# A hybrid decoder trunk: the attention's branch product two query/key stages later, gate weights one stage earlier, embedding transposes later

## The chip, the core and the metric

The kernel runs on one core of a Trainium2 chip. The metric is the device time of one execution in microseconds (us). TensorE (PE; its weight loads PEld) multiplies, ScalarE (ACT) and VectorE (DVE) work element by element, GpSimd (POOL) does a few small steps, and SyncE (SP) issues the transfers from memory.

## The reference

Two layers over 256 tokens of width 1024; all inputs are float32. Cut to what matters here:

```python
h = h + 0.5 * swiglu(rmsnorm(h, ffn1_norm), ...)
u = rmsnorm(h, mix_norm);  z = u @ w_in     # split: m_qk, m_v, m_o, m_i, m_f, a_q, a_k, a_v, g_m, g_a
m_qk = silu(causal_dwconv(m_qk))            # 4 taps
hm = sigmoid(m_o) * headnorm(mlstm(m_q, m_k, m_v, m_i, logsigmoid(m_f)))    # 4 heads of 256
ha = sliding-window attention with sinks(norm(a_q), norm(a_k), a_v)         # 16 heads of 64, window 128
h = h + (sigmoid(g_m) * (hm @ w_branch_m) + sigmoid(g_a) * (ha @ w_branch_a)) @ w_out
h = h + 0.5 * swiglu(rmsnorm(h, ffn2_norm), ...)
h = h + sigmoid(rmsnorm(h, ple_norm) @ ple_gate_w) * (p_i @ ple_proj_w)
```

## The kernel before

Every float32 operand of a large product is split in two: a high part (a cast on ScalarE, `wh` for weights) and a low part (a subtraction on VectorE, `wl`). A product is then three matmuls per tile: high by high, high by low, low by high. Weights come in megabytes: SP loads one into one of two `raw` buffers, and ScalarE and VectorE split each half of it into one of eight ring slots of `wh` and `wl`. A raw buffer is loaded again when its second half is split.

The order of the instructions on TensorE, ScalarE, VectorE and SP is written by the program while it is built. `self.jobs` holds the stages in turn: each is a function that issues one stage's matmuls. Side work runs in chains (generators), of which one step is issued between matmuls when `Clock`, the planner's own estimate of every engine's time, says that its input is ready; `tick` looks for such steps. Weight splits are issued in the same way (`feed`). So a stage that is moved in `jobs` also moves the loads of its weights on SP, their splits, and the places of the chains around it. A wait in the chip comes where the planner's clock was too early.

In the mixer (`mix`) the stages of one layer are, with the tile names of the profile: `kvq` (attention keys, values and queries), `v` (the recurrence's values), `gt` (merge gate A), `if` (input and forget gates, `log_gates`), `ya` (the attention's branch product), `z` twice (the recurrence's queries and keys of heads 0 and 1, each followed by the chain `conv`), `og` (output gate), `z` twice (heads 2 and 3), `gt` (merge gate M), `ym`, `yo`.

Chains that run beside them: the attention groups (`sc` scores, `pr` probabilities, `tp` their transposes, `ptd` the split transposes, `ha` the outputs, which are split into the tiles `qT`, the operand of `ya`); `scans`, from the `if` product through Exp and Ln and VectorE's scans to `gcols` and `rows`; `decays` (`wt`, then Exp into `w`); `conv` (`cv` taps, `cy` the Silu, `qk` its split); and one `head` per head (`st`, `num`, `og`, `tp`, `hmT`). The matmuls of `if` take a 128x1024 tile `wif`, which `gate_weights` (line 905) clears on POOL and fills with two casts and two subtractions.

In the last block of a layer (`ple`) the embedding `p` is loaded by a prelude that the down product before it calls when it begins. `later_T` schedules p's transposes; its last argument is the earliest time by the planner's clock.

## Time and profile before

| | us |
|---|---|
| median of 3 runs (1392.11 to 1394.45) | 1393.32 |
| profiled execution | 1395.02 |
| its span, first to last instruction | 1393.2 |
| TensorE busy | 1371.4 |
| ScalarE busy | 726.7 |
| VectorE busy | 862.3 |

The mean granted TensorE clock is 0.997. In the rows that follow, a line of a timeline is start, duration, engine, what is written from what, the form, the count, and in brackets the idle time just before and what ended it. A row of stretches has the width, then the busy time of TensorE, its weight loads, VectorE, ScalarE and GpSimd with the instructions in brackets, then the granted clock, the share of the transfer engines, and GB/s. All instructions that the planner records have line 130.

### The profile page before, as it was taken

How to read it: one execution, taken by the hardware profiler on the slowest of the kernel's cores; microseconds unless marked ns; L12 is line 12 of the kernel's file. 1: busy time of each engine (PE TensorE's matmuls, PEld its weight loads, DVE VectorE, ACT ScalarE, POOL GpSimd, SP SyncE). 2: the span in 40 equal slices, each digit the busy share in tenths (PEclk: the TensorE clock that was granted, in tenths of full speed). 3: DMA queues.
4: the chain of work that ended last, by engine and by line, in shares of the span. 5: the costliest groups of instructions: out<-in, count | busy, mean ns of one | idle time of the engine just before them, and what ended most of it. 6: DMA issues, size and time to landing. Idle time of an engine off the chain costs nothing.

```text
span 1393.2 us, 21942 instructions
## 1 busy us (share of the span) xinstructions
PE 1371.4 (98%) x9056; PEld 1236.9 (89%) x9056; DVE 862.3 (62%) x1213; ACT 726.7 (52%) x1138; POOL 55.0 (4%) x84
## 2 busy tenths in 40 slices
PE   8999999999999999999999999999999999999998
PEld 5999887899899889988779998878998998999886
DVE  5655457765886665554575554586658876555544
ACT  5555346874665454443554443477756554544433
POOL 0000012000000000000000000120000000000000
PEclk9999999999999999999999999999999999999999
DMA  6665645464545565565456566455445554655551
GB/s 209 218 210 167 228 136 196 124 149 151 168 152 182 166 212 186 169 229 182 165 164 210 172 207 208 143 164 145 135 134 192 173 160 161 227 191 170 205 181 61
DMA packets 125830, 243.81 MB, mean 175 GB/s; under 512 B 14977, under 2 KB 23841, under 8 KB 125730
## 3 DMA queue, kind: packets, MB, share of 16 engines
q1 hardware_dynamic: 125730, 242.41, 54.6%
q8 instruction: 71, 1.16, 0.4%
q14 instruction: 29, 0.24, 0.0%
HBM read 241.34 MB, written 1.05 MB: 174 GB/s over the span
## 4 chain that ended last, share of the span: by engine, by line
PE 90%; DMA 3%; DVE 3%; ACT 2%; issue 1%; POOL 0%; SPq 0%; ACTq 0%; POOLq 0%
PE dn L130 16%; PE pg L130 15%; PE pu L130 14%; PE gu L130 7%; PE z L130 7%; PE gt L130 6%; PE ya L130 4%; PE ym L130 3%; PE v L130 3%; PE og L130 3%; PE yo L130 3%; PE kvq L130 3%; PE tp L130 2%; PE sc L130 1%; DVE wl L130 1%; PE ha L130 1%
## 5 line engine op out<-in xcount | busy, mean ns | idle before, releaser
L130 DVE TENSOR_TENSOR wl<-raw,wh 128x1024 fp32r<-128x1024 f32 (+1 forms) x448 | 540.8, 1222 | 365.8 <-ACT wh L130 364.7
L130 ACT CAST wh<-raw 128x1024 fp32r<-128x1024 f32 x448 | 461.5, 1050 | 439.8 <-PE dn L130 86.9
L130 PE MATMUL dn<-wh,hid 128*128 128x512 f32 x688 | 218.4, 395 | 0.0
L130 PE MATMUL pg<-uT,wh 128*128 128x256 f32 x1088 | 194.6, 281 | 0.0
L130 PE MATMUL pu<-uT,wh 128*128 128x256 f32 x1088 | 193.6, 281 | 0.0
L130 PEld LDWEIGHTS pg<-uT,wh 128*128 128x128 f32 x1088 | 167.1, 189 | 0.2
L130 PEld LDWEIGHTS pu<-uT,wh 128*128 128x128 f32 x1088 | 166.9, 188 | 0.0
L130 PEld LDWEIGHTS dn<-wh,hid 128*128 128x128 f32 x688 | 129.3, 188 | 29.9
L130 PE MATMUL pg<-uT,wl 128*128 128x256 f32 x544 | 152.9, 281 | 0.0
L130 PE MATMUL pu<-uT,wl 128*128 128x256 f32 x544 | 152.9, 281 | 0.0
L130 PE MATMUL dn<-wl,hid 128*128 128x512 f32 x352 | 138.7, 394 | 0.0
L130 PEld LDWEIGHTS pu<-uT,wl 128*128 128x128 f32 x544 | 102.5, 188 | 0.0
L130 PEld LDWEIGHTS pg<-uT,wl 128*128 128x128 f32 x544 | 102.4, 188 | 0.0
L130 PE MATMUL gt<-uT,wh 128*128 128x256 f32 x512 | 93.2, 283 | 0.0
L130 PE MATMUL z<-uT,wh 128*128 128x256 f32 x512 | 92.1, 282 | 0.0
L130 PE MATMUL gu<-wh,uT 128*128 128x512 f32 x256 | 83.5, 402 | 1.9 <-ACT uT L130 1.9
L130 PEld LDWEIGHTS gt<-uT,wh 128*128 128x128 f32 x512 | 79.0, 188 | 1.2
L130 PEld LDWEIGHTS dn<-wl,hid 128*128 128x128 f32 x352 | 66.2, 188 | 15.3
L130 PEld LDWEIGHTS z<-uT,wh 128*128 128x128 f32 x512 | 78.7, 188 | 0.2
L130 PE MATMUL z<-uT,wl 128*128 128x256 f32 x256 | 72.0, 281 | 0.0
L130 PE MATMUL gt<-uT,wl 128*128 128x256 f32 x256 | 71.9, 281 | 0.0
L130 PE MATMUL kvq<-wh,uT 128*128 128x512 f32 x192 | 63.7, 401 | 0.0
(194 smaller groups left out, 2034.2 us busy)
## 6 DMA issues: line engine op xcount, KB each, us to landing
raw<-in_w_in_dram SPq DMA_DIRECT2D x60, 1024.0 KB, 5.1
raw<-in_ffn_w_up_dram SPq DMA_DIRECT2D x40, 1024.0 KB, 5.2
raw<-in_ffn_w_down_dram SPq DMA_DIRECT2D x40, 1024.0 KB, 5.5
raw<-in_ffn_w_gate_dram SPq DMA_DIRECT2D x39, 1024.0 KB, 5.7
raw<-in_w_branch_a_dram SPq DMA_DIRECT2D x16, 512.0 KB, 5.9
raw<-in_w_branch_m_dram SPq DMA_DIRECT2D x8, 1024.0 KB, 5.1
raw<-in_w_out_dram SPq DMA_DIRECT2D x8, 1024.0 KB, 5.1
raw<-in_ple_gate_w_dram SPq DMA_DIRECT2D x8, 1024.0 KB, 7.3
```

Of the source, the lines that this page charges most:

```text
L130: return issue(*args, **kw)
```

## The change

Three edits. The two query/key jobs of heads 0 and 1 are put ahead of the attention's branch product instead of behind it, so that `ya` stands two `z` stages farther back. `gate_weights` becomes a job of its own ahead of the gate stage, and keeps its tile in `w_if`, where `log_gates` takes it. And p's transposes may start 15 us after their issue by the planner's clock, not 5.

```diff
-                self.later_T(p[:, t, :], pT, 0, t, 2, self.clock.now + 5.0)
+                self.later_T(p[:, t, :], pT, 0, t, 2, self.clock.now + 15.0)
...
+        self.jobs.append(rec.gate_weights)
         ga = gate(C_GA)
 
         self.jobs.append(rec.log_gates)
+        for part in range(2):
+            rec.qk_job(w_in, part, 0)
...
         job_T(units_a, att.haT, "ya", use_a, lambda: self.finish(groups[0]))
 
-        for part in range(2):
-            rec.qk_job(w_in, part, 0)
         units_o = self.pair(w_in, C_O)
...
-        return w
+        self.w_if = w
 
     def log_gates(self):
         tr, nc = self.tr, self.nc
-        w = self.gate_weights()
-        ps = tr.bank("if")[:, :T]
+        w, ps = self.w_if, tr.bank("if")[:, :T]
```

On TensorE in layer 0, around the last attention outputs (`ha`) before the change; `qT26` and `qT28` are the high and the low part of the second half of their split result, `qT25` and `qT27` of the first half.

```order
L130 MATMUL ya578_3165<-qT25_136,wl553_2990 128x256
L130 MATMUL ha585_3229<-ptd588_3253,vpad368_1994 128x512 x3
L130 MATMUL ha585_3229<-ptd589_3255,vpad368_1994 128x512 x3
L130 MATMUL tp597_3340<-ident_79,gates572_3159 128x4
...
L130 MATMUL ya575_3162<-qT26_137,wh555_3013 128x256
L130 MATMUL ya575_3162<-qT28_139,wh555_3013 128x256
L130 MATMUL ya575_3162<-qT26_137,wl556_3014 128x256
```

And after it; the rows left out are the rest of the second `z` job with the gates' transposes and three of the `wt`, and then the first half of `ya` with the fourth.

```order
L130 MATMUL z578_3163<-uT6_117,wl554_2993 128x256
L130 MATMUL ha580_3185<-ptd587_3271,vpad368_1994 128x512 x3
L130 MATMUL z595_3335<-uT5_116,wh556_3015 128x256
...
L130 MATMUL ya614_3503<-qT25_136,wh584_3228 128x256
L130 MATMUL ya614_3503<-qT27_138,wh584_3228 128x256
...
L130 MATMUL ya614_3503<-qT26_137,wh605_3422 128x256
L130 MATMUL ya614_3503<-qT28_139,wh605_3422 128x256
```

The last `ha` moved from five small transposes ahead of the first reader of `qT26` to a whole `z` job and half of `ya` ahead of it.

On ScalarE at the same place before the change, from the split of that `ha` result through the decays (`em` and `w` are Exp).

```order
L130 CAST qT26_137<-ha585_3229 128x4x128
L130 ACT_TABLE_LOAD
L130 ACTIVATE em600_3358<-gcols598_3346 128x8
L130 ACTIVATE w602_3370<-wt601_3360,gcols598_3346 128x128 x3
L130 CAST wh604_3390<-raw594_3320 128x1024
L130 ACTIVATE w602_3370<-wt603_3386,gcols598_3346 128x128 x3
```

And after it, with the Silus of the convolutions (`cy`) of the moved jobs.

```order
L130 CAST qT26_137<-ha580_3185 128x4x128
L130 ACT_TABLE_LOAD
L130 ACTIVATE em602_3394<-gcols600_3366 128x8
L130 ACTIVATE w604_3412<-wt603_3396,gcols600_3366 128x128 x3
L130 CAST wh605_3422<-raw592_3313 128x1024
L130 ACT_TABLE_LOAD
L130 ACTIVATE cy608_3435<-cv593_3329 128x512
L130 ACT_TABLE_LOAD
L130 ACTIVATE w604_3412<-wt607_3431,gcols600_3366 128x128 x3
L130 ACT_TABLE_LOAD
L130 ACTIVATE cy609_3453<-cv594_3332 128x512
L130 CAST qk610_3467<-cy608_3435 128x512
```

The Exp of the decays and the Silu of the convolutions now alternate, with a table load at each turn; in all there are 18 table loads in the program where 10 were.

On TensorE in the down product before `ple` in layer 0 before the change, the transposes of `p`:

```order
L130 MATMUL dn1021_6444<-wh996_6264,hid41_152 128x512
L130 MATMUL dn1021_6444<-wl997_6265,hid41_152 128x512
L130 MATMUL dn1021_6444<-wh996_6264,hid47_158 128x512
L130 MATMUL tp1027_6482<-ident_79,p1017_6439 128x128 x2
L130 MATMUL tp1028_6485<-ident_79,p1017_6439 128x128 x2
```

and after it:

```order
L130 MATMUL dn1021_6444<-wh1009_6369,hid42_153 128x512
L130 MATMUL dn1021_6444<-wl1010_6370,hid42_153 128x512
L130 MATMUL dn1021_6444<-wh1009_6369,hid48_159 128x512
L130 MATMUL tp1037_6550<-ident_79,p1017_6439 128x128 x2
L130 MATMUL tp1038_6553<-ident_79,p1017_6439 128x128 x2
```

They stand 48 matmuls of the down product farther back. On SP the load of `p` stays where it was; in the mixer the four megabytes for the two moved `z` jobs are now loaded ahead of the four for `ya`.

## The prediction

> **What bounds the kernel now.** First the page: the span, the engines and the chain that ended last.

> ```profile
> span 1393.2 us, 21942 instructions
> PE 1371.4 (98%) x9056; PEld 1236.9 (89%) x9056; DVE 862.3 (62%) x1213; ACT 726.7 (52%) x1138; POOL 55.0 (4%) x84
> PE 90%; DMA 3%; DVE 3%; ACT 2%; issue 1%; POOL 0%; SPq 0%; ACTq 0%; POOLq 0%
> ```

> TensorE works 98% of the span and carries 90% of the chain, so a change in order that adds and removes no matmul can win only what TensorE loses: its idle 21.8 us (1393.2 less 1371.4), and time at a reduced clock, which hides inside "busy". Next the list of TensorE's waits (us in total, times, longest) for the waits that the change touches.

> ```profile
> PE ya L130 <- DVE qT L130: 2.7, 2, 1.3
> PE tp L130 <- DMA p<-in_p_dram: 2.1, 2, 1.7
> PE sc L130 <- DVE ptd L130: 0.9, 2, 0.5
> PE ya L130 <- ACT qT L130: 0.6, 2, 0.3
> PE if L130 <- DVE wif L130: 0.4, 2, 0.2
> ```

> All come in pairs, one per layer. Four of the five belong to the three edits: `ya` (the branch product), `if` (the gate weights' product), `tp` from `p` (the embedding transposes). These lists count idle time from the modelled end of a matmul; what a stall costs must be taken from start to start, and its stage looked at for the clock.

> **The branch product.** Timeline of TensorE in layer 0 (start, duration), then stretches (width, busy per engine, granted clock), then both for layer 1.

> ```profile
> 319.52 0.38 PE L130 MATMUL ya<-qT,wh 128*128 128x256 f32 x1 [0.28 <-ACT qT L130]
> 321.25 0.39 PE L130 MATMUL ya<-qT,wh 128*128 128x256 f32 x1 [1.34 <-DVE qT L130]
> ...
> 321.30:322.50 1.20, 1.20 (x9) 1.10 (x10) 0.00 (x0) 0.05 (x1) 0.00 (x0) 0.91 0.57 97
> 322.50:324.00 1.50, 1.50 (x8) 1.50 (x8) 0.00 (x0) 0.83 (x3) 0.00 (x0) 0.50 1.00 380
> 324.00:326.00 2.00, 2.00 (x13) 2.00 (x11) 0.00 (x0) 0.00 (x0) 0.00 (x0) 0.57 0.48 185
> 335.70:358.40 22.70, 22.70 (x193) 22.70 (x193) 15.19 (x21) 12.47 (x17) 0.00 (x0) 1.00 0.48 154
> ...
> 1008.61 0.39 PE L130 MATMUL ya<-qT,wh 128*128 128x256 f32 x1 [0.28 <-ACT qT L130]
> 1010.34 0.39 PE L130 MATMUL ya<-qT,wh 128*128 128x256 f32 x1 [1.34 <-DVE qT L130]
> 1011.50:1013.00 1.50, 1.50 (x11) 1.50 (x10) 0.00 (x0) 0.88 (x3) 0.00 (x0) 0.59 0.95 348
> 1013.00:1015.00 2.00, 2.00 (x11) 2.00 (x10) 0.00 (x0) 0.06 (x1) 0.00 (x0) 0.50 0.57 222
> 1015.00:1020.00 5.00, 5.00 (x43) 4.71 (x43) 2.73 (x4) 3.59 (x8) 0.00 (x0) 0.98 0.01 3
> ```

> A 256-column matmul takes its turn every 0.118 us (22.70 for 193, in the stage after). In layer 0 the second half of `ya` waits 0.28 for the high part of qT, and from 319.52 to 321.25 for the low part: 1.73 less 0.118 is 1.61. Right behind it the clock falls: 1.20 x 0.09 + 1.50 x 0.50 + 2.00 x 0.43 = 1.72 lost. Layer 1: 0.28, 1.73 less 0.118 = 1.61, and 1.50 x 0.41 + 2.00 x 0.50 + 5.00 x 0.02 = 1.72. Together 3.61 a layer, 7.2 us, twice what the list of waits shows.

> After the change two query/key jobs (384 matmuls, 45 us) stand between the gate product and `ya`. The last `ha`, which makes qT's second half, is issued in the middle of them, and `ya` first reads that half 23 us later. So this stall goes, and I count all of its 7.2.

> [...]

> **The gate weights.** Two casts (ScalarE) and two subtractions (VectorE) on 128x32 move from just ahead of the `if` product to the start of the gate stage, with POOL's 128x1024 memset.

> ```profile
> 300.81 0.28 PE L130 MATMUL gt<-uT,wl 128*128 128x256 f32 x1
> 301.31 1.19 PE L130 MATMUL if<-uT,wif 128*128 128x256 f32 x8 [0.21 <-DVE wif L130]
> 989.87 0.28 PE L130 MATMUL gt<-uT,wl 128*128 128x256 f32 x1
> 990.38 1.19 PE L130 MATMUL if<-uT,wif 128*128 128x256 f32 x8 [0.23 <-DVE wif L130]
> ```

> Start to start 0.50 and 0.51, less 0.118: 0.38 and 0.39, 0.8 us together. In their new place they stand ahead of ScalarE's exponentials of scores. They are 0.34 us of work there, and ScalarE idles 0.58 before its next cast of a transposed tile, as the two rows of ScalarE's timeline say (the first in its old place):

> ```profile
> 300.59 0.34 ACT L130 CAST wif<-wif 128x32 fp32r<-128x32 f32 x2
> 272.34 0.59 ACT L130 CAST ptd<-tp 128x512 fp32r<-128x512 f32 x1 [0.58 <-PE tp L130]
> ```

> so the push ends there, and I cost it at nothing; without that cover it would come back as at most 0.34 a layer. POOL's memset takes another buffer of the pool, which the order shows free since a transpose in the value stage, ahead of the whole gate stage; on POOL's queue nothing stands behind it until the heads' powers in the output-gate stage.

> **The embedding transposes.** They go back from 5 to 15 us behind p's load by the planner's clock; in the order that is 48 matmuls of 512 columns.

> ```profile
> 611.95 0.40 PE L130 MATMUL dn<-wh,hid 128*128 128x512 f32 x1
> 612.75 0.63 PE L130 MATMUL tp<-ident,p 128*128 128x128 f32 x4 [0.40 <-DMA p<-in_p_dram]
> 1300.96 0.40 PE L130 MATMUL dn<-wh,hid 128*128 128x512 f32 x1
> 1303.03 0.63 PE L130 MATMUL tp<-ident,p 128*128 128x128 f32 x4 [1.68 <-DMA p<-in_p_dram]
> ...
> 1303.73 0.39 PE L130 MATMUL dn<-wl,hid 128*128 128x512 f32 x1
> 1303.96 0.63 PE L130 MATMUL dn<-wh,hid 128*128 128x512 f32 x2
> ```

> A 512-column matmul turns in 0.235 (1303.73 to 1303.96 and its like), so the losses are 0.80 less 0.235 = 0.57, and 2.07 less 0.235 = 1.84: 2.4 us. 48 of them are 11.3 us of new cover against 1.84: the wait goes. p's load itself keeps its place on SP's queue; pT is first read by the next block, behind the whole down product, so its cast and subtraction have room.

> **What it adds.** The matmuls are the same. ScalarE now meets the Exp of the decays between the Silus of the convolutions: the order has 7 table loads in each mixer stage where 3 were, 18 against 10 in all.

> ```profile
> L130 ACT ACT_TABLE_LOAD x10 | 12.8, 1283 | 10.0 <-DVE cv L130 5.3 <-PE gu L130 3.9 <-PEq L1271 0.7
> 319.49 1.28 ACT L130 ACT_TABLE_LOAD   x1
> 320.78 0.21 ACT L130 ACTIVATE em<-gcols 128x8 f32<-128x8 f32 x1
> L130 ACT CAST wh<-raw 128x1024 fp32r<-128x1024 f32 x448 | 461.5, 1050 | 439.8 <-PE dn L130 86.9
> L130 DVE TENSOR_TENSOR wl<-raw,wh 128x1024 fp32r<-128x1024 f32 (+1 forms) x448 | 540.8, 1222 | 365.8 <-ACT wh L130 364.7
> L130 DVE SCALAR_TENSOR_TENSOR cv<-z,feat,cv 128x255 f32<-128x255 f32 (+2 forms) x96 | 44.9, 480 | 8.1 <-ACT cv L130 5.8
> raw<-in_w_in_dram SPq DMA_DIRECT2D x60, 1024.0 KB, 5.1
> 372.59 2.00 ACT L130 CAST wh<-raw 128x1024 fp32r<-128x1024 f32 x2 [2.46 <-DMA raw<-in_w_in_dram]
> ```

> Four more are 5.1 us of ScalarE a layer, and some loads hold the queue until VectorE has done its taps (0.48 each). What is late next? I walked the new order of layer 0 with these durations. `if` now starts at 300.93 and ends at 303.3. The query job takes 22.7 for its products and 3 for the `ha` and `tp` between; the last `ha` stands at 317.5 and its operand is subtracted at 314.3 (VectorE does the gate scans until 312.5, then one wl and the subtraction): 3.2 to spare. The `ya` job starts at 331.0 and reads qT's second half from 342.7; that is written at 322.9. ScalarE's stretch with the loads begins at 320.4: load and `em` 321.8, first decays (their `wt` ends at 322.5) and a wh 324.4, load and Silu 326.2, load and decays 328.3, load, Silu and a cast 330.7, four `cv` 332.6, load and decays 334.6, a cast and wh of `ya`'s sixth part 336.2. VectorE, held by twelve taps until 337.5 and one subtraction, has its wl at 339.3, wanted at 345.5: 6.2 to spare. The low part of the first keys (343.0) is wanted by `st` at 348.4: 5.4. The first output-gate weights are split at 347.6, wanted at 356.7. So the loads cost nothing on TensorE. Their cover is these 5.4 us, about one layer's extra loads again.

> The SP queue now loads four megabytes of query/key weights ahead of the four branch weights. With two raw buffers and 5.1 us a landing the branch weights arrive 10 us or more before `ya`.

> Behind that the heads of the recurrence stand closer to their inputs, and the walk finds little room: 1.5 us at the first head's transpose in the output-gate stage and at the third head's `st`, 1.2 at its `num`, about 0 at the second head's transpose (388.1 against 388.05). A landing that is 2.46 late, as the last row shows ScalarE waiting, would turn one of these into a wait. Bounds: nothing; or a wait like `ya`'s, 3.6 a layer. Since most margins are over 1 us I take 0.5 a layer, near the small `sc` wait (0.9 for two).

> **Sum** against the profiled execution (1395.02, of which the span is 1393.2): -7.2 - 0.8 - 2.4 + 1.0 = -9.4, so 1385.6. The median of the runs shown, 1393.32, is 1.7 below that execution; by the same step it becomes 1383.9, and I say 1384.0.

> **Rivals.**

> First, the slow clock does not belong to the wait of `ya`, and strikes elsewhere. For it: in layer 1 TensorE lost 1.84 at p's transposes, as much as at `ya`, and the clock stayed. [...] Against: both layers show it 0.9 to 1.2 us behind `ya`'s wait, nowhere else in a busy stretch. Then 3.4 of the gain stays out: 1387.3.

> Second, one of the heads' thin margins becomes a wait of 1.6 us and drags the clock down again, in each layer: 7.2 back in place of my 1.0, so 1390.1. For it: the margins of 0 to 1.5; against: the same chains stand in the order of before, and the list of waits has none of their tiles.

> Third, the change doesn't do what it says: `ya` waits for something new, such as its own later weights, 5 us a layer. 1393.3 less 10.4 plus 10 is 1393, no difference.

> Fourth, slower: ScalarE's added table loads. If the queue runs later than the 6.2 and 5.4 of cover, `ya` and `st` wait for it, us for us, with 1.7 of slow clock. To lose 3 us in all it must eat 10.4 + 3, 6.7 a layer, hence run some 10 us later than walked, twice the 5.1 that the loads take. Time 1396 to 1398. [...]

> **Chances.** The forecast as it stands 0.66, the clock rival 0.09, the heads' waits 0.12, no effect 0.07, slower 0.06. The measurement of this kernel can tell about 0.2% (2.8 us). The heads' case lies at 3.2 and is split, 0.10 faster and 0.02 same: faster 0.85, same 0.09, slower 0.06. Range: the top takes in the heads' case, 1390.2; the bottom has no new wait (1.0), the two `sc` waits gone by shift (0.9), and 1 of the runs' spread (1392.11 to 1394.45): 1381.0.

> **What would show it.** Right: no wait of `ya` for qT, clock 1.00 through both `ya` stages, `if` 0.118 behind the last `gt`, no wait for p; 18 table loads; spans shorter by 3 to 4 a layer in the mixer. Wrong: a new TensorE wait of over 1 us on `hmT`, `og`, `num`, `st` or `wl` in the mixer, or a clock under 0.9 there.

## The result, and the profile after

The changed kernel takes 1381.52 us (median of 5 runs, 1379.98 to 1383.27) against 1392.52 for the kernel before (5 runs, 1391.37 to 1394.45): a ratio of 0.992, 95% interval 0.9907 to 0.9934. That is 11.0 us less, where 9.4 were forecast (1384.0, range 1381.0 to 1390.2). It is faster, and a little more than said. The times of the kernel before that follow leave out one run of the first set, which took 2248.49 us at a granted clock of 0.558.

The page of the changed kernel, its first lines and the shares of the chain that ended last:

```profile
span 1381.5 us, 21941 instructions
PE 1366.2 (99%) x9056; PEld 1233.3 (89%) x9056; DVE 860.7 (62%) x1213; ACT 734.8 (53%) x1146; POOL 55.4 (4%) x84
PE 96%; DMA 1%; DVE 1%; ACT 1%; issue 0%; POOL 0%; SPq 0%; ACTq 0%; POOLq 0%
```

The matmuls are as many as before. TensorE's idle time went from 21.8 to 15.3 us (1381.5 less 1366.2), and its busy time fell by 5.2, though no matmul was removed. That part is pace (how closely the matmuls follow each other), the clock (0.997 granted before, 0.998 after) and short gaps that count as busy. Next its waits, the whole list (us in total, times, longest):

```profile
PE tp L130 <- DVE xn L130: 3.9, 2, 3.0
PE g L130 <- DVE pick L265: 2.4, 1, 2.4
PE gu L130 <- ACT uT L130: 2.2, 1, 2.2
PE sc L130 <- DVE ptd L130: 0.9, 2, 0.5
PE gu L130 <- DVE wl L130: 0.8, 1, 0.8
```

The waits of `ya` for qT, of `if` for wif and of `tp` for p are gone, all three, and no wait of the heads (`hmT`, `og`, `num`, `st`) came. At the places themselves, from TensorE's timeline and, for `ya`, the stretches from its start to the output gate in both layers:

```profile
300.92 0.28 PE L130 MATMUL gt<-uT,wl 128*128 128x256 f32 x1
301.04 0.40 PE L130 MATMUL if<-uT,wif 128*128 128x256 f32 x2
...
331.53 0.40 PE L130 MATMUL ya<-qT,wh 128*128 128x256 f32 x2
331.77 0.28 PE L130 MATMUL ya<-qT,wl 128*128 128x256 f32 x1
331.50:357.40 25.90, 25.90 (x222) 25.80 (x221) 19.03 (x29) 18.26 (x29) 0.00 (x0) 1.00 0.49 160
1015.00:1041.00 26.00, 26.00 (x222) 25.90 (x221) 18.98 (x29) 18.25 (x29) 0.00 (x0) 1.00 0.49 158
...
618.14 0.39 PE L130 MATMUL dn<-wh,hid 128*128 128x512 f32 x1
618.37 0.60 PE L130 MATMUL tp<-ident,p 128*128 128x128 f32 x4
```

`if` starts 0.12 behind the last `gt`; the `ya` stage runs 25.90 of 25.90 us at clock 1.00 (it began at 331.5, where the walk of the prediction had 331.0, and `og` at 357.3, where it had 356.7); p's transposes stand between two matmuls of `dn` without a gap.

### The profile page after: what moved, and what is told of

Same layout as the page of the kernel before. It is cut to its first block, busy times and chain, and to the rows that moved or that the text cites. A ratio compares the mean times of both kernels' runs of the same rounds, so it can differ in the third digit from the quotient of the medians.

```text
span 1381.5 us, 21941 instructions
## 1 busy us (share of the span) xinstructions
PE 1366.2 (99%) x9056; PEld 1233.3 (89%) x9056; DVE 860.7 (62%) x1213; ACT 734.8 (53%) x1146; POOL 55.4 (4%) x84
## 4 chain that ended last, share of the span: by engine, by line
PE 96%; DMA 1%; DVE 1%; ACT 1%; issue 0%; POOL 0%; SPq 0%; ACTq 0%; POOLq 0%
PE dn L130 17%; PE pg L130 16%; PE pu L130 14%; PE gu L130 7%; PE z L130 7%; PE gt L130 7%; PE kvq L130 5%; PE ya L130 3%; PE v L130 3%; PE ym L130 3%; PE yo L130 3%; PE og L130 3%; PE tp L130 3%; PE sc L130 1%; PE ha L130 1%; DMA raw<-in_ffn_w_gate_dram 1%
## 5 line engine op out<-in xcount | busy, mean ns | idle before, releaser
L130 DVE TENSOR_TENSOR wl<-raw,wh 128x1024 fp32r<-128x1024 f32 (+1 forms) x448 | 540.2, 1222 | 351.3 <-ACT wh L130 348.5
L130 ACT CAST wh<-raw 128x1024 fp32r<-128x1024 f32 x448 | 460.5, 1050 | 414.1 <-PE dn L130 82.9
L130 PE MATMUL dn<-wh,hid 128*128 128x512 f32 x688 | 218.1, 395 | 0.0
L130 PE MATMUL pg<-uT,wh 128*128 128x256 f32 x1088 | 194.0, 281 | 0.0
L130 PE MATMUL pu<-uT,wh 128*128 128x256 f32 x1088 | 192.9, 280 | 0.0
L130 PEld LDWEIGHTS pg<-uT,wh 128*128 128x128 f32 x1088 | 166.4, 188 | 0.2
L130 PEld LDWEIGHTS pu<-uT,wh 128*128 128x128 f32 x1088 | 166.2, 188 | 0.0
L130 PEld LDWEIGHTS dn<-wh,hid 128*128 128x128 f32 x688 | 129.2, 188 | 30.2
L130 PE MATMUL pg<-uT,wl 128*128 128x256 f32 x544 | 152.4, 280 | 0.0
L130 PE MATMUL pu<-uT,wl 128*128 128x256 f32 x544 | 152.2, 280 | 0.0
L130 PE MATMUL dn<-wl,hid 128*128 128x512 f32 x352 | 139.0, 395 | 0.0
L130 PEld LDWEIGHTS pu<-uT,wl 128*128 128x128 f32 x544 | 102.4, 188 | 0.0
L130 PEld LDWEIGHTS pg<-uT,wl 128*128 128x128 f32 x544 | 102.3, 188 | 0.0
L130 PE MATMUL z<-uT,wh 128*128 128x256 f32 x512 | 93.5, 284 | 0.0
L130 PE MATMUL gt<-uT,wh 128*128 128x256 f32 x512 | 93.1, 283 | 0.0
L130 PE MATMUL gu<-wh,uT 128*128 128x512 f32 x256 | 83.4, 402 | 2.2 <-ACT uT L130 2.2
L130 PEld LDWEIGHTS gt<-uT,wh 128*128 128x128 f32 x512 | 78.8, 188 | 1.2
L130 PEld LDWEIGHTS dn<-wl,hid 128*128 128x128 f32 x352 | 66.1, 188 | 15.1
L130 PEld LDWEIGHTS z<-uT,wh 128*128 128x128 f32 x512 | 78.8, 188 | 0.6
L130 PE MATMUL z<-uT,wl 128*128 128x256 f32 x256 | 71.9, 281 | 0.0
L130 PE MATMUL gt<-uT,wl 128*128 128x256 f32 x256 | 71.8, 280 | 0.0
L130 PE MATMUL kvq<-wh,uT 128*128 128x512 f32 x192 | 63.7, 401 | 0.0
## 6 DMA issues: line engine op xcount, KB each, us to landing
raw<-in_w_in_dram SPq DMA_DIRECT2D x60, 1024.0 KB, 5.1
raw<-in_ffn_w_up_dram SPq DMA_DIRECT2D x40, 1024.0 KB, 5.1
raw<-in_ffn_w_down_dram SPq DMA_DIRECT2D x40, 1024.0 KB, 5.2
raw<-in_ffn_w_gate_dram SPq DMA_DIRECT2D x39, 1024.0 KB, 5.5
raw<-in_w_branch_m_dram SPq DMA_DIRECT2D x8, 1024.0 KB, 5.1
raw<-in_w_out_dram SPq DMA_DIRECT2D x8, 1024.0 KB, 5.2
raw<-in_ple_gate_w_dram SPq DMA_DIRECT2D x8, 1024.0 KB, 8.0
```

The lines of the kernel that those rows point to most:

```text
L130: return issue(*args, **kw)
```

## The experiments

Eleven runs in three sets, each set on a chip of its own. Each ratio is to the kernel before, run on the same chip in the same set: its median is 1391.7 in the first set and 1391.78 in the second. The third set, the kernel before itself, has one execution of each run.

**One edit at a time.** `e_ya_only` has the query/key jobs moved ahead of the branch product's units and the two other edits undone:

```
+        for part in range(2):
+            rec.qk_job(w_in, part, 0)
...
-        for part in range(2):
-            rec.qk_job(w_in, part, 0)
```

> Only the two query/key jobs are moved ahead of the branch product; gate weights and embedding transposes stay as before. Theory (the wait of ya carries the slow clock with it): 3.6 us a layer go, idle 1.9 and slow clock 1.7, so 7.2 us less than before (1385.3), no wait of ya for qT, clock 1.00 through z, ya and og; the 0.4 ahead of if and the waits for p stay. Rival (the slow clock is not tied to that wait): only the idle time goes, 3.8 us less (1388.7), and the clock still falls to 0.5 somewhere in the mixer.

Measured: 1385.58 (1384.63 to 1389.07), ratio 0.9958, interval 0.9943 to 0.9974: about -6 (-3.6 to -7.9). The wait of `ya` is gone, and its profile has no slow stretch up to the last matmul. The time alone does not decide between the theory's 7.2 and the rival's 3.8: both lie inside the interval, the second near its edge.

`e_wif_only` has only the gate weights put together ahead of the gate stage (and kept in `w_if`, as in the change):

```
+        self.jobs.append(rec.gate_weights)
         ga = gate(C_GA)
```

> Only the gate weights are put together one stage ahead. Theory: the 0.38 us ahead of if go in each layer, 0.8 us less (1391.7), which the measurement cannot tell from no change; the waits of ya and the slow clock behind them stay. Rival: what if no longer waits for, ya waits longer for (its qT hangs on the transposes of pr beside it): no change at all, ya's wait 0.4 longer.

Measured: 1391.40 (1388.64 to 1393.08), ratio 0.9991, interval 0.9981 to 1.0002. The sign cannot be told from the time; in the list of waits that of `if` is gone and that of `ya` stays, no longer than before (3.2 in all, where the first profile of before has 3.3).

`e_p_only` has only the later transposes of p:

```
-                self.later_T(p[:, t, :], pT, 0, t, 2, self.clock.now + 5.0)
+                self.later_T(p[:, t, :], pT, 0, t, 2, self.clock.now + 15.0)
```

> Only the embedding transposes are moved back. Theory: TensorE's waits for p go, 0.57 us in layer 0 and 1.84 in layer 1, but layer 0's is given back at the handover from the embedding block to the next layer, where TensorE waits for the gate weights and not for itself: 1.8 to 2.4 us less (1390.1 to 1390.7). Rival (the changed kernel's 2.0 in layer 1 and the rest of its gain came from the mixer): under 1 us.

Measured: 1389.44 (1387.87 to 1390.21), ratio 0.9981, interval 0.9971 to 0.9991: -2.6 by the ratio, where its term said -2.4. Whether layer 0's part is given back at the handover to layer 1 cannot be read from it, because the wait for `xn` there changes by more than that part from profile to profile. The three ratios add to -0.70%, the whole change has -0.8%; so within the intervals the edits add up and none needs another.

This run also held the first surprise. It keeps both waits of `ya`, but behind them, where the first profile of before had half the clock, it has all of it:

```profile
319.49 0.39 PE L130 MATMUL ya<-qT,wh 128*128 128x256 f32 x1 [0.28 <-ACT qT L130]
321.22 0.38 PE L130 MATMUL ya<-qT,wh 128*128 128x256 f32 x1 [1.34 <-DVE qT L130]
...
321.00:323.00 2.00, 1.78 (x15) 1.69 (x16) 0.16 (x1) 0.58 (x3) 0.00 (x0) 1.00 0.61 138
323.00:325.00 2.00, 2.00 (x20) 1.90 (x19) 0.00 (x0) 0.82 (x3) 0.00 (x0) 1.00 1.00 384
```

**One stage instead of two.** `e_one_stage` is the changed kernel with only the query job ahead of the branch product's units, the key job behind them as before:

```
+        rec.qk_job(w_in, 0, 0)
...
-        for part in range(2):
-            rec.qk_job(w_in, part, 0)
+        rec.qk_job(w_in, 1, 0)
```

> As the changed kernel, but only the query job stands ahead of the branch product, the key job behind it as before: 96 matmuls, 11.4 us of cover in place of 22.7. Theory: the last ha stands about 14 us ahead of the first reader of qT's second half, which needs 5.4 (from 317.5 to 322.9 in the walk); no wait, the same time as the changed kernel within 0.2% (1381.5). Rival: the gate scans on VectorE hold ptd back so that half the cover does not do: ya waits again, 2 to 4 us a layer, 1385 to 1389.

Measured: 1383.61 (1382.36 to 1385.32), ratio 0.9944, interval 0.9929 to 0.9959. One stage is enough to take the wait away: `ya` starts at 317.45 and its list of waits has no `ya`. Whether the second stage gives something on top (0.992 against 0.9944) the intervals leave open.

**What sets off the slow clock.** In the second set the changed kernel was run again, and two of its kin in which only the place of p's transposes differs, so that TensorE waits for p's load for a time that can be chosen (the first added line is `a_p_at_0`, the second `a_p_at_3`). The expectations name two theories: by theory A a wait sets off the slow clock once it is long enough, by theory B the slow clock falls where it falls, whatever waits.

```
-                self.later_T(p[:, t, :], pT, 0, t, 2, self.clock.now + 15.0)
+                self.later_T(p[:, t, :], pT, 0, t, 2, self.clock.now + 0.0)
+                self.later_T(p[:, t, :], pT, 0, t, 2, self.clock.now + 3.0)
```

> The changed kernel once more, so that the three others of this set are compared on the same chip. Theory: 1381.5 within 1.5, mean granted clock about .999 (the kernels without the branch product's wait averaged .9988 so far, those with it .9980), 0.992 of before. If the clock's average over runs is no property of the kernel, the mean will be as near .998 as .999.

Measured: 1380.92 (1379.70 to 1381.87), ratio 0.9921, interval 0.9908 to 0.9933: the result once more, in another set. Mean clock of its runs .9988.

> The same transposes at 3 us: 15 matmuls of the down product stand ahead of them, so TensorE waits about 2.7 (layer 0) and 3.9 us (layer 1). Idle alone: +6.1 over the changed kernel, 1387.6. Theory A with the price seen behind the branch product's waits of 1.9 us in before: slow clock behind both, 1391. [...] Theory B: 1387.6.

Measured: 1391.26 (1390.04 to 1392.22), +10.3 on `a_again`; the profiled run itself 1390.04. Idle alone was put at 6.1; by the timeline the two down products take 8.4 of the 10.3 (2.7 and 5.7, from the first `dn` to the first `pp`), a slow stretch in layer 1 among it. The two waits, and the 2 us stretches behind each:

```profile
607.49 0.63 PE L130 MATMUL tp<-ident,p 128*128 128x128 f32 x4 [2.43 <-DMA p<-in_p_dram]
607.00:609.00 2.00, 1.51 (x9) 1.37 (x10) 1.42 (x3) 0.65 (x2) 0.00 (x0) 1.00 0.94 285
609.00:611.00 2.00, 2.00 (x11) 1.59 (x10) 0.09 (x1) 0.70 (x1) 0.00 (x0) 1.00 0.46 186
...
1294.38 0.63 PE L130 MATMUL tp<-ident,p 128*128 128x128 f32 x4 [3.92 <-DMA p<-in_p_dram]
1294.00:1296.00 2.00, 1.62 (x9) 1.42 (x10) 0.76 (x2) 1.17 (x3) 0.00 (x0) 0.91 1.00 406
1296.00:1298.00 2.00, 2.00 (x6) 1.55 (x5) 1.23 (x1) 0.42 (x1) 0.00 (x0) 0.50 0.08 33
1298.00:1300.00 2.00, 2.00 (x8) 1.61 (x7) 0.60 (x1) 1.05 (x1) 0.00 (x0) 0.74 0.00 0
```

A wait of 2.43 us left the clock at 1.00; one of 3.92 was followed by half the clock for 2.00 x 0.18 + 2.00 + 2.00 x 0.52 = 3.4 us (at half speed a stretch counts twice what its mean clock lacks from 1).

> Embedding transposes of the changed kernel at 0 instead of 15 us behind p's load by the planner's clock: they stand ahead of the down product. p lands 6.2 (layer 0) and 7.4 us (layer 1) after that product begins, so TensorE idles about that long. Idle alone: +13.2 over the changed kernel, 1394.7. Theory A (a wait sets off the slow clock once it is long enough): both waits are the longest of the whole kernel outside its ends, both are followed by about 3.4 us at half clock, +1.7 each, 1398, with rows of 10 us at about .83 right behind the waits. Theory B (the slow clock falls where it falls, whatever waits): 1394.7, clock near 1.00 behind the waits.

Measured: 1399.21 (1398.41 to 1401.24), ratio 1.0056, interval 1.0043 to 1.0068: +18.3 on `a_again`, more than theory A's 16.6 and far from theory B's 13.2.

```profile
606.78 1.09 PE L130 MATMUL tp<-ident,p 128*128 128x128 f32 x4 [5.90 <-DMA p<-in_p_dram]
602.00:604.00 2.00, 0.00 (x0) 0.00 (x0) 2.00 (x2) 0.54 (x2) 0.00 (x0) 0.79 1.03 424
604.00:606.00 2.00, 0.00 (x0) 0.00 (x0) 0.44 (x2) 0.00 (x0) 0.00 (x0) 0.50 1.04 381
606.00:608.00 2.00, 1.22 (x5) 1.25 (x6) 0.12 (x1) 0.47 (x2) 0.00 (x0) 0.50 0.89 320
608.00:610.00 2.00, 2.00 (x6) 1.52 (x5) 0.73 (x2) 0.28 (x1) 0.00 (x0) 0.50 0.54 209
```

Here the half clock begins inside the wait, at 603.2 (2.00 x 0.42 = 0.84 ahead of 604), and ends at 610.0: 6.8 us, twice 3.4. In layer 1, behind a wait of 7.48, it is again 6.8. In each layer some 3.4 of it lie behind the wait, on matmuls, and cost half of that: the second FFN and its down product took 17.0 us more than in `a_again` over both layers, of which 5.90 + 7.48 = 13.4 are idle. So in these two profiles the slow clock came in pieces of 3.4 us, once 3.4 and twice 6.8, each in or behind a wait, and theory B is out.

**The same wait, three more times.** The kernel before, unchanged, profiled three times over.

> The kernel before, unchanged, profiled again: its two waits of the branch product (0.28 + 1.34 us idle each) are there in every run. Theory A (the wait itself sets off the half clock): 2 us stretches at 0.50 to 0.57 behind both waits, as in the first profile, granted clock .997. Theory C (the clock is set for whole stretches of 3.4 us that begin at a moment of their own, and a wait of 1.6 us counts only where it falls well inside one): the half clock shows behind some of the waits and not behind others; from the mean clocks (.9981 over 61 runs with these waits, .9988 over 27 without) about 0.55 such stretches a run are due to them, so about one wait in four, and a run without any reads .999 to 1.000 and is 3 us shorter than the first profile.

Measured: 1390.38 us. Both `ya` waits are there. Behind that of layer 0 the clock stays, behind that of layer 1 it halves:

```profile
320.00:322.00 2.00, 1.79 (x15) 1.70 (x16) 0.15 (x1) 0.60 (x3) 0.00 (x0) 1.00 0.62 145
322.00:324.00 2.00, 2.00 (x20) 1.90 (x19) 0.00 (x0) 0.82 (x3) 0.00 (x0) 1.00 0.99 385
...
1003.92 0.39 PE L130 MATMUL ya<-qT,wh 128*128 128x256 f32 x1 [0.28 <-ACT qT L130]
1005.65 0.38 PE L130 MATMUL ya<-qT,wh 128*128 128x256 f32 x1 [1.34 <-DVE qT L130]
1006.00:1008.00 2.00, 2.00 (x12) 1.80 (x11) 0.00 (x0) 0.52 (x3) 0.00 (x0) 0.50 0.92 245
1008.00:1010.00 2.00, 2.00 (x13) 2.00 (x13) 0.00 (x0) 0.37 (x2) 0.00 (x0) 0.67 0.73 280
```

> The same once more: Theory A two slow stretches behind the branch product's waits; Theory C none to two, not the same number in each run, and the time goes with their number, 1.7 us each.

Measured: 1390.81 us; no slow stretch between the first clock record, at 16.4, and the last matmul.

> The same a third time: Theory A two slow stretches behind the branch product's waits; Theory C none to two, and over the three profiles fewer than six in all.

Measured: 1388.85 us; none either, and a span of 1387.0 against 1393.2 in the first profile of before.

Theory A falls in its plain form. Theory C, that the clock is set for stretches of 3.4 us which begin at moments of their own, agrees with these profiles, with two misses in its numbers. It expected a slow stretch behind one wait in four; with the first profile of before (2 of 2), `e_wif_only` (2 of 2) and `e_p_only` (0 of 2), the slow clock followed 5 of 12 such waits. And it expected the time to go with the number of slow stretches; the spans are 1388.6 with one and 1389.0 and 1387.0 with none, because the wait for `xn` was longest (3.00 us) in `b_again_2`.

The clock records of the traces show where these stretches, or windows, lie. In each of the thirteen profiles every change of the clock stands a whole number of 3.413 us behind the first one (in the first profile of before at 307.2, 310.6, 996.7, 1000.1 and 1375.6 us behind it: 90, 91, 292, 293 and 403 windows; in `after` at 679.25, 682.67 and 1365.33: 199, 200 and 400). With edges at that distance drawn through the whole span, the idle time between two of them can be counted. In the first profile of before the half clock of layer 0 began at 322.3; the window ahead of it, from 318.88, holds both gaps of `ya`, 1.62 us. In `a_p_at_3` the wait of 3.92 is cut into 1.76 and 2.16; the half clock came behind the second part only. The wait of 2.43 there is cut at 606.14 into 1.08 and 1.35, and a wait of 3.00 for `xn` in `b_again_2` at 695.61 into 1.7 and 1.3 (its rows stand at the end): the clock stayed at 1.00 behind both. A reading that fits these cases, and that no run shows by itself, is that the idle time within one window goes with the clock of the next, and that a wait which an edge cuts has only its part in each.

How much idle time went with it? The idle time of the lists does not tell the cases apart, because it starts at the modelled end of a matmul: behind the 1.62 of `ya` the clock halved, behind 1.79 ahead of a transpose in `e_wif_only` it did not.

```profile
693.23:696.64 3.41, 1.62 (x8) 1.01 (x8) 2.52 (x5) 1.71 (x5) 0.55 (x1) 1.00 0.17 64
696.64:700.05 3.41, 3.40 (x19) 2.73 (x18) 1.70 (x3) 2.90 (x4) 0.00 (x0) 1.00 0.02 5
```

Counted from start to start, each matmul with its usual turn in these traces (0.118 for 256 columns, 0.232 for 512, 0.109 for a transpose of 128), the cases come apart. Up to the last matmul of the first profiles of before and after, some 800 windows, the three that lost 2.05, 2.14 and 3.18 us were followed by half clock, and no other was, up to a loss of 1.70. Over all thirteen profiles, some 5200 windows, by the same count the 12 that lost 2.05 us or more were all followed by half clock, and no other was, up to a loss of 2.02. These losses are an estimate from the start times, too coarse to trust the 0.03 between the nearest cases. What the chip itself counts, and whether it has a limit there, these runs do not show. The two gaps of `ya` span 2.0 us (319.24 to 321.25). If the edges fall anywhere with the same chance, they come whole between two of them, 3.4 apart, with 1.4 / 3.4 = 0.41; that is an estimate from these two lengths, and 5 of 12 is 0.42.

**ScalarE's table loads.** `a_tanh` leaves out the SiLU of the convolutions and has Tanh in its place, so that the eight added table loads go:

```
-        nc.scalar.activation(y, acc.rearrange("p c t -> p (c t)"), AF.Silu)
+        nc.scalar.activation(y, acc.rearrange("p c t -> p (c t)"), AF.Tanh)
```

> Leaves out the convolutions' SiLU: Tanh stands in its place, which shares its table with the Exp of the decays, so ScalarE loads 10 tables instead of 18 (the changed kernel's 8 added loads of 1.28 us are gone). Theory (the loads lie in ScalarE's cover): same as the changed kernel within 0.2%, ScalarE's busy time down by about 10 us. Rival four of the prediction (table loads cost TensorE time, even if below what it forecast): faster by 1 to 5 us.

Measured: 1382.49 (1381.68 to 1383.08), ratio 0.9933, interval 0.9920 to 0.9945. From the lists of groups, the loads of `a_again` and then of `a_tanh`:

```profile
L130 ACT ACT_TABLE_LOAD x18 | 23.1, 1283 | 4.9 <-PE gu L130 3.9 <-PEq L1271 0.7
...
L130 ACT ACT_TABLE_LOAD x10 | 12.8, 1283 | 4.7 <-PE gu L130 3.9 <-PEq L1271 0.7
```

ScalarE does 10.3 us less in loads (734.6 to 725.5 busy in all), and the time does not fall (1382.49 against 1380.92 for `a_again`). The loads were covered.

## Why the prediction was right, and where its numbers were not

The clearest pair of profiles is one in which the clock records show no slow stretch up to the last matmul: `b_again_3` for before and `a_again` for after. They are one execution each, on different chips.

```profile
span 1387.0 us, 21942 instructions
PE 1368.7 (99%) x9056; PEld 1234.4 (89%) x9056; DVE 862.3 (62%) x1213; ACT 727.3 (52%) x1138; POOL 54.0 (4%) x84
...
span 1377.9 us, 21941 instructions
PE 1364.0 (99%) x9056; PEld 1231.9 (89%) x9056; DVE 860.6 (62%) x1213; ACT 734.6 (53%) x1146; POOL 55.7 (4%) x84
```

9.1 us, with no slow stretch in either. The table goes stage by stage, from the first matmul of a stage to the first of the next by the timeline. For the mixer of layer 1 these are, in `b_again_3` and in `a_again`:

```profile
952.65 0.40 PE L130 MATMUL gt<-uT,wh 128*128 128x256 f32 x2
1166.00 0.39 PE L130 MATMUL gu<-wh,uT 128*128 128x512 f32 x1
...
948.50 0.40 PE L130 MATMUL gt<-uT,wh 128*128 128x256 f32 x2
1159.63 0.40 PE L130 MATMUL gu<-wh,uT 128*128 128x512 f32 x1
```

The differences are 213.35 and 211.13.

| stretch | before | after | gain | forecast at full clock |
|---|---|---|---|---|
| mixer, layer 0 (`gt` to `gu`) | 213.72 | 210.72 | 3.00 | 2.27 (ya 1.89, if 0.38) |
| mixer, layer 1 | 213.35 | 211.13 | 2.22 | 2.28 (ya 1.89, if 0.39) |
| second FFN up to `dn`, layer 0 | 123.22 | 122.78 | 0.44 | 0 |
| the same, layer 1 | 123.46 | 122.55 | 0.91 | 0 |
| `dn` to `pp`, layer 0 | 62.22 | 61.61 | 0.61 | 0.57 |
| `dn` to `pp`, layer 1 | 63.74 | 61.73 | 2.01 | 1.84 |
| the rest | 587.29 | 587.38 | -0.1 | +1.0 allowed for waits, 0 |

**The branch product, idle part.** Right: 1.89 a layer forecast; the whole of layer 1's mixer gives 2.22 with `if`. In layer 0 0.7 more came than forecast; by tiles, each matmul counted up to the next start, `ya` gave 1.92, `if` and its gate stage about 0.4, the small transposes 0.35 (the wait of 0.28 for the high part of qT stands behind them) and `ym` 0.63, while `z` took 0.57 longer; for `ym` no run shows a cause.

**The branch product, clock part.** The mis-sized term. The prediction took 1.72 a layer, 3.44 in all, out of one profile in which half clock followed both waits. Behind 12 such waits there were 5 slow stretches, each worth 1.5 (the mixer of layer 0 took 215.27 with one and 213.7 without): 1.3 us a run, not 3.44. The mean clocks of all runs say about as much: .9981 over 61 runs of kernels with the wait, .9988 over 27 without, and .0007 of 1390 is 1.0, give or take 0.6. So the first rival was right in its price, roughly (2 to 2.5 of the 3.4 stay out), though not in its words: the slow clock did stand behind the wait, but only 5 times in 12. My ground against it, "both layers show it", was two draws of that chance. (The slow stretches there began 1.0 and 1.4 behind the end of the wait, not 0.9 to 1.2; nothing hangs on it.) The other ground, that the clock stayed behind 1.84 at p's transposes, fits the windows: an edge at 1301.92 cut that wait, the window ahead of it lost 0.76 and the one behind it 1.24, and the clock read 1.00 from 1298.50 to 1308.74. In `b_again_1` the same wait lay whole in one window, which lost 1.99, and the clock stayed there too.

**The gate weights.** Right: the 0.38 and 0.39 are in the mixer's sums above, and the wait of `if` is gone. The casts in their new place cost nothing that shows.

**The embedding transposes.** Right: 0.61 and 2.01 for 0.57 and 1.84.

**The allowance for new waits,** 1.0, was not needed: the waits after hold none of the heads' tiles, so the second rival did not come, thin as the margins of the walk were. Its error was small (the walk's start of `ya` was 0.5 early, of `og` 0.6).

**Not seen at all:** 1.35 in the second FFN stages, 0.44 and 0.91, alike in `after` and `a_again` and absent in the four profiles of before. In layer 0 `e_wif_only` and `e_ya_only` each show it alone (122.78 and 122.75), in layer 1 `e_ya_only` does (122.80) and `e_wif_only` does not (123.34), nor does `e_one_stage` (123.44). No wait stands there in either list. What it is stays open.

So -9.4 came about as -7.0 of idle, -3.44 of clock and +1.0; measured it is -9.1 of idle and pace and about -1 of clock, and the rest of the 11.0 is inside the interval (-9.2 to -12.9). The mechanism, waits that go, was right; that the number came so near was partly luck: a term that was 2 too large stood against an allowance that was 1 too careful and a gain of some 2 that it didn't see.

One statement of the prediction is wrong as it stands: the two query/key jobs ahead of `ya` are not 384 matmuls and 45 us but 192 and 22.7, as its own walk has it a few lines on. By the walk `ya` starts 13.5 us behind the last `ha` and reads its second half 25 us behind it, and the conclusion stands.

**The other rivals.** No effect: out, nothing in `ya` waits for its weights. Slower through table loads: out, `a_tanh`.

**Where the clock went instead.** In the profile of the changed kernel one slow stretch stands at the handover to layer 1's first FFN; the same kernel's second profile has none there. First `after`, where the wait lies whole in one window, then `a_again`:

```profile
693.93 1.45 PE L130 MATMUL tp<-ident,xn 128*128 128x128 f32 x6 [2.98 <-DVE xn L130]
690.66:694.07 3.41, 0.43 (x3) 0.14 (x2) 2.40 (x5) 1.82 (x5) 0.55 (x1) 1.00 0.24 91
694.07:697.49 3.42, 3.42 (x13) 3.00 (x13) 1.85 (x3) 2.23 (x4) 0.00 (x0) 0.50 0.02 5
...
690.95 1.32 PE L130 MATMUL tp<-ident,xn 128*128 128x128 f32 x8 [1.52 <-DVE xn L130]
692.00:694.00 2.00, 2.00 (x12) 1.65 (x11) 1.36 (x2) 1.92 (x4) 0.00 (x0) 1.00 0.03 8
```

This wait of the transposes for `xn` is in both kernels, 1.4 to 3.0 us in the profiles of before and after, and is the largest that is left: with its clock it costs, by estimate from these rows, up to 4.7 (3.0 and half of 3.4).

## What to carry to other kernels

A stall's idle time can be read from one profile, start to start; what the clock takes behind it cannot: here half clock followed 5 of 12 like waits. Read two or three profiles of the same kernel before a slow stretch is written down as the price of a wait, and multiply by how often it comes. In these traces the changes of the clock lay whole multiples of 3.413 us apart, and edges drawn at that distance told the waits that lay whole between two of them from those that were cut. Where work is moved over a whole stage to hide a wait, walk the new order of every engine that feeds it: the walk here named the places rightly, and its thin margins held.

## What the runs showed of the hardware that was not expected

```profile
696.91 1.32 PE L130 MATMUL tp<-ident,xn 128*128 128x128 f32 x8 [3.00 <-DVE xn L130]
692.19:695.61 3.42, 1.72 (x8) 1.07 (x6) 2.24 (x5) 1.21 (x3) 0.55 (x1) 1.00 0.72 269
695.61:699.02 3.41, 2.10 (x13) 1.69 (x14) 2.71 (x5) 2.06 (x5) 0.00 (x0) 1.00 0.00 0
699.02:702.43 3.41, 3.41 (x16) 2.80 (x15) 1.68 (x3) 2.22 (x3) 0.00 (x0) 1.00 0.02 5
```

And a wait's name is not always its cause: in `b_again_2` and `b_again_3` the 1.7 us of layer 1's p transposes are put down to VectorE's `wl`, where the first profile has the load of p; the move of those transposes removes it under either name.

In these profiles the clock column says nothing of the first microseconds: ahead of the first record, at 12 to 17 us, it reads 1.00, but there a matmul of 512 columns turns in 0.43 (`a_again`, 10.32 to 10.75), nearly twice the 0.232 of later. In `b_again_3` and `a_again` this makes no difference to the comparison: from the first `gu` to the first `pg` both take 26.49.
